# Per-head factors spread by one product for two heads, low-rank factors padded to 128 rows, and two smaller edits in a three-layer fp32 kernel

## The chip, the cores and the metric

The kernel runs as one program on one core of a Trainium2 chip. The metric is the device time of one execution in microseconds (us). PE is the engine of matrix products, DVE the vector engine, ACT the engine of activation functions, POOL the general engine, and SP a queue that only starts transfers (DMAs). Everything is in fp32 precision for 1024 tokens of 1024 features.

## The reference, cut to what matters

Three layers run one after another: a gated linear recurrence ("hawk"), an RWKV7 time mix, and a hybrid of a convolution and a diagonal state space (S5). The first two are each followed by a gated feed-forward part (FFN) and a per-layer embedding. Of the RWKV7 layer this matters here, with 16 heads of 64 features:

```python
w = w0 + tanh(xw @ w1) @ w2          # w1: 1024 x 64, w2: 64 x 1024
a = sigmoid(a0 + (xa @ a1) @ a2)     # a1: 1024 x 64, a2: 64 x 1024
g = sigmoid(xg @ g1) @ g2            # g1: 1024 x 160, g2: 160 x 1024
kk = k * k_k;  kk = kk / norm of kk over each head's 64 features
y = rwkv7_scan(r, decay(w), k, v, -kk, kk * a)     # token after token, per head
yn = (y - mean) * rsqrt(var + eps)                 # mean and variance over each head
out = ((yn * ln_w + ln_b) + bonus) * g @ w_o
```

The state space of the third layer takes `dt = exp(log_dt)`, one value for each of 32 groups. Each layer begins with `x * rsqrt(mean(x*x) + eps) * gain` over the 1024 features of a token.

## The kernel before, in words

Activations lie feature-major: a tile has 128 features on the partitions and 512 tokens (a "half") or 256 (a "segment") along it. A large product is three products in a row (mm3, lines L249, L250, L251), since each operand is split into two parts of 12 bits. Small products are plain fp32, and the trace then shows two records for each: a row with x2 is one product.

**Start.** Token rows of the input are loaded by SP in the order of the program, with some 25 small parameter rows (L204) between them, and transposed on PE (L356). The copies of the transposed tiles (L2130) are squared by ACT (L309, L312), and DVE adds eight squares (L313). PE sums them over the partitions (L273), DVE and POOL take the root (L289, L290), PE spreads the result (L281, in rstd_bcast), DVE multiplies (L328), and ACT and DVE split the result and the weights (L215, L216). Then the first products run. The second half of the tokens repeats this later.

**The woven stage** (some 1340 to 2420 us) is the RWKV7 layer. Generators yield steps, each with an engine and an estimated time, and a planner (weave_, L686) writes their instructions in one order for all engines. The engines then take them strictly in this order. Three kinds of work are woven: the projections (mm3 with 256 tokens; weights and activations prepared by DVE and ACT), the "finish" of each pair of heads and segment (8 pairs x 4 segments = 32 times), and the scan over 16 chunks of 64 tokens, with its closing part "post" for each chunk. Behind the scan comes the product with w_o.

In a finish the second low-rank factors are applied: lwD holds them in DRAM as three slots of 128 rows, w2 over a2 in slot 0, g2[0:128] in slot 1, and g2[128:160] on rows 96 to 127 of slot 2. fload (L931) loads a pair's part, and lora2 (L923) multiplies only the rows in use:

```python
zw = lora2(pz, lw, [(0, 0, 0, 64)])                # 64 rows
za = lora2(pz, lw, [(0, 0, 64, 128)])              # 64 rows
zo = lora2(pz, lw, [(1, 1, 0, P), (2, 2, 96, P)])  # 128 rows and 32 rows
```

The norm of kk: ACT squares k (L986), PE sums over each head (heads_sum, L1431) into one column per head with tokens on the partitions, DVE forms rn (L991, L992), and heads_bcast (L1434) spreads the factors back over 64 features each. Its stationary operand is one column, read 64 times; two products, one for each head, fill 128 output rows:

```python
self.nc.tensor.matmul(bc[64 * hd : 64 * hd + 64, c * P : (c + 1) * P],
                      x[:, 2 * c + hd : 2 * c + hd + 1].to_broadcast([P, 64]), self.ident,
                      start=True, stop=True)
```

L1003 writes t1 over the squared k, and L1007 multiplies t1 by the spread factors. In post the same helper spreads the root of the variance: PE centres y (L1303), ACT squares and copies (L1306, L1308), PE sums (L1431), DVE and POOL form the factor hr (L1315), heads_bcast spreads it with eight products, and DVE closes (L1319 to L1324).

**The end of the stage.** The last chunk has the inverse of small triangular blocks (DVE, L1146 and L1149), whose result goes through DRAM: SP stores it (L1157, four transfers) and loads it turned (L1168), and PE goes on with L1179. At about the same time s5_prep (L1444) begins: POOL issues its parameter loads (L1475 to L1481), the last two of which read every second element of log_dt into 64 partitions each.

Of the kernel before, what the change touches and what calls it, by code (L numbers as in the profile page):

```python
# [8 lines left out]
F32 = mybir.dt.float32  # L9
# [47 lines left out]
class Net:  # L57
    """Feature-major activations: tile [128 features, 512 tokens] per (k, half)."""
# [34 lines left out]
    def open_top(self):  # L93
        """One more pool above the group's, closed before them."""
# [4 lines left out]
    def open_rtop(self):  # L99
        """Another one, from the other end of the memory."""  # L100
# [44 lines left out]
    def s(self, dt=F32, n=HT):  # L145
        """scratch [128, n <= 516]"""
# [3 lines left out]
    def extra(self, tag, shape, dt, every, bufs):  # L150
        """now and then a slot of the pool on the right, where that is for more of the others"""
# [7 lines left out]
    def ld(self, src=None, n=HT, rows=P):  # L159
        """tile for a load; loads have slots of their own, for they run ahead"""  # L160
# [66 lines left out]
    def load_ws(self, srcs, nk, m, tag="w"):  # L227
        """srcs: DRAM APs arranged [p, nk, n] for columns c..c+n; returns hi, lo tiles [P, nk, m]"""
# [17 lines left out]
    def mm3(self, ps, w, x, first, last):  # L246
        """ps += w.T @ x with w = (hi, lo), x = (hi, lo)"""
# [5 lines left out]
    # W columns [c0, c0+128) for all nk row tiles  # L253
# [3 lines left out]
    def lin(self, w, xs, nk):  # L257
        """xs: list of (hi, lo) per k -> PSUM tile"""
# [6 lines left out]
    def rstd_bcast(self, acc, scale, eps, acc2=None):  # L265
        """acc [128, 512] -> PSUM [128, 512]: (sum over partitions * scale + eps)^-0.5 on all partitions; with acc2,
        for which that is the factor of another norm: that one and the product of both"""
# [25 lines left out]
        rs = root(sums(acc))  # L293
# [8 lines left out]
    def square(self, h, k, half, gain=None):  # L302
        """h[k][half] is final: its part of the sum of squares (and of that of the products with the gain)"""
# [54 lines left out]

    def load_T(self, src, nk, sink):
# [4 lines left out]
    def blocks(self, nblk, units, in_unit, post, nk_out, wout, h, add_bias=None, lag=2, delay=3, mid=None, late=None, fill=None, nlate=LATE):  # L364
        """units: weight items per block; in_unit(b, i, half, w) ; post(b, half) -> list of nk_out (hi, lo)"""
# [51 lines left out]
        # the first half of the last block before the second half of the one before it  # L417
# [34 lines left out]
    def hawk(self, h, xn, mid, late):  # L452
# [5 lines left out]
        # c8 = 8 softplus(-lam), softplus(z) = max(z, 0) + log1p(exp(-|z|)), log1p(e) = 2 atanh(e / (2 + e))  # L458
# [100 lines left out]
    def ple_prep(self, layer):  # L559
        """p, features on the partitions, split"""  # L560
# [40 lines left out]
    NSEG, SN = 4, 256  # token segments of the dense part  # L601

    def rwkv_consts(self):
# [7 lines left out]
        # block-diagonal ones (2 heads), identity minus the same / 64, and per-head selector columns  # L611
# [8 lines left out]
        # [s, t] masks on both heads: s < t | s <= t  # L620
# [1665 lines left out]
```

## Time and profile before

| | |
|---|---|
| three runs, us | 4186.73, 4188.85, 4215.79 |
| median, us | 4188.85 |
| span of the profiled execution, us | 4186.6 |
| busy PE / DVE / ACT / POOL, us | 3949.4 / 2544.7 / 1466.1 / 179.3 |
| mean granted clock of PE, share of full speed | 0.957 |

For the profiled execution the page gives its span, from the first to the last instruction, and no other time; the span is 0.13 us below the fastest of the three runs and 2.25 us below the median. PE is busy for 94% of the span. Times in the trace count from the span's start.

### The profile page before, as it was taken

The numbers are of one execution on the slowest core, as the hardware profiler recorded it, in microseconds if no ns is written. First come the engines' busy times: TensorE is split into PE (matmuls) and PEld (weight loads), VectorE is DVE, ScalarE is ACT, GpSimd is POOL, SyncE is SP. The second block draws the span as 40 slices with busy tenths as digits, with TensorE's granted clock in tenths as the row PEclk, the third lists the DMA queues.
The fourth block names the chain that finished last, engine by engine and source line by source line (L and its number), as shares of the span: only waits on it lengthen the run. The fifth ranks groups of instructions, "written<-read, shape, count | busy, mean of one in ns | idle before, by whom it ended". The sixth has DMA issues, their size and how long they took to land.

```text
span 4186.6 us, 58441 instructions
## 1 busy us (share of the span) xinstructions
PE 3949.4 (94%) x22510; PEld 3216.6 (77%) x22510; DVE 2544.7 (61%) x5192; ACT 1466.1 (35%) x2491; POOL 179.3 (4%) x376
## 2 busy tenths in 40 slices
PE   6998999999988999999999699999999999999899
PEld 5776788888877877777867587888887877888687
DVE  6665733333364678777756476354536599997655
ACT  4455511111132665554542241111113332222533
POOL 0000000000000000000000101010100000000000
PEclk8999999999998999989979799999999999999999
DMA  3111111111122789676776541212211244332775
GB/s 103 48 47 34 51 46 51 41 56 51 34 67 88 216 252 237 174 209 170 194 194 173 97 127 52 63 49 66 63 49 58 71 119 118 109 115 96 236 226 186
DMA packets 695830, 464.49 MB, mean 111 GB/s; under 512 B 197956, under 2 KB 620800, under 8 KB 695552
## 3 DMA queue, kind: packets, MB, share of 16 engines
q1 hardware_dynamic: 514272, 367.80, 30.0%
q10 hardware_dynamic: 175872, 83.90, 7.3%
q0 software_dynamic: 5408, 9.06, 1.1%
q8 instruction: 177, 2.90, 0.3%
q14 instruction: 101, 0.83, 0.1%
HBM read 355.51 MB, written 106.69 MB: 110 GB/s over the span
## 4 chain that ended last, share of the span: by engine, by line
PE 69%; DVE 12%; DMA 7%; ACT 5%; issue 4%; SPq 1%; POOL 1%; ACTq 0%; DVEq 0%; POOLq 0%
PE mm L249 15%; PE mm L251 14%; PE mm L250 14%; PE ob L249 4%; PE ob L250 4%; PE ob L251 4%; DVE cy L1882 3%; PE g L1100 2%; PE g L926 1%; PE g L1438 1%; PE y L1291 1%; DMA BK<-bkD 1%; PE y L1289 1%; DVE w L863 1%; PE mm L2073 1%
## 5 line engine op out<-in xcount | busy, mean ns | idle before, releaser
L249 PE MATMUL mm<-T,w 128*128 128x512 f32 (+1 forms) x2944 | 1152.6, 393 | 47.1 <-ACT w L215 22.5
L251 PE MATMUL mm<-T,w 128*128 128x512 f32 (+1 forms) x2944 | 1149.9, 391 | 9.6 <-DVE w L216 9.6
L250 PE MATMUL mm<-T,w 128*128 128x512 f32 (+1 forms) x2944 | 1150.3, 392 | 1.1 <-DVE T L1380 0.9
L249 PEld LDWEIGHTS mm<-T,w 128*128 128x128 f32 x2944 | 558.6, 190 | 174.3 <-ACT w L215 26.9
L251 PEld LDWEIGHTS mm<-T,w 128*128 128x128 f32 x2944 | 559.0, 190 | 126.8 <-DVE w L216 12.1
L250 PEld LDWEIGHTS mm<-T,w 128*128 128x128 f32 x2944 | 559.7, 190 | 117.5 <-DVE T L1380 1.7
L215 ACT CAST w<-wraw 128x1024 fp32r<-128x1024 f32 (+1 forms) x286 | 288.4, 1014 | 988.8 <-PE mm L250 700.2
L216 DVE TENSOR_TENSOR w<-wraw,w 128x1024 fp32r<-128x1024 f32 (+1 forms) x286 | 335.1, 1177 | 373.9 <-ACT w L215 371.1
L389 DVE TENSOR_TENSOR h<-ob,h 128x512 f32<-128x512 f32 x416 | 286.1, 690 | 230.7 <-PE ob L251 227.5
L249 PE MATMUL ob<-S,w 128*128 128x512 f32 x896 | 359.2, 401 | 21.7 <-DVE h L389 21.1
L1882 DVE SCALAR_TENSOR_TENSOR cy<-cu,pv,cy 128x512 f32<-128x512 f32 x480 | 350.9, 749 | 12.3 <-ACT cy L1880 2.6
L250 PE MATMUL ob<-S,w 128*128 128x512 f32 x896 | 354.7, 396 | 0.2 <-DVE S L216 0.2
L251 PE MATMUL ob<-S,w 128*128 128x512 f32 x896 | 354.7, 396 | 0.0
L249 PE MATMUL mm<-M,w 128*128 128x256 f32 x768 | 255.1, 332 | 16.4 <-ACT M L837 8.5
L250 PE MATMUL mm<-N,w 128*128 128x256 f32 x768 | 229.7, 299 | 4.4 <-DVE N L839 4.3
L251 PE MATMUL mm<-M,w 128*128 128x256 f32 x768 | 229.8, 299 | 4.3 <-DVE w L863 4.0
L249 PEld LDWEIGHTS ob<-S,w 128*128 128x128 f32 x896 | 169.9, 190 | 70.2 <-DVE h L389 30.2
L251 PEld LDWEIGHTS ob<-S,w 128*128 128x128 f32 x896 | 169.7, 189 | 38.6
L250 PEld LDWEIGHTS ob<-S,w 128*128 128x128 f32 x896 | 170.1, 190 | 36.3 <-DVE S L216 0.6
L249 PEld LDWEIGHTS mm<-M,w 128*128 128x128 f32 x768 | 157.0, 204 | 50.3 <-issue 23.3
L439 DVE TENSOR_TENSOR S<-mm,S 128x512 f32<-128x512 f32 x88 | 60.8, 690 | 211.7 <-PE mm L251 209.8
L215 ACT CAST S<-S 128x512 fp32r<-128x512 f32 x128 | 79.3, 620 | 266.3 <-DVE S L439 154.4
(458 smaller groups left out, 5431.9 us busy)
## 6 DMA issues: line engine op xcount, KB each, us to landing
wraw<-in_rw_w_rkv_dram ACTq DMA_DIRECT2D x96, 512.0 KB
wraw<-in_ffn_w_in_dram SPq DMA_DIRECT2D x88, 512.0 KB
wraw<-in_w_in_dram SPq DMA_DIRECT2D x48, 512.0 KB
wraw<-in_ffn_w_out_dram SPq DMA_DIRECT2D x44, 512.0 KB
BK<-bkD SPq DMA_DIRECT2D x64, 256.0 KB
wraw<-in_rw_w_o_dram ACTq DMA_DIRECT2D x24, 512.0 KB
wraw<-in_lru_w_in_dram SPq DMA_DIRECT2D x20, 512.0 KB
wraw<-in_ple_w_gate_dram SPq DMA_DIRECT2D x16, 512.0 KB
```

The source lines that it names most:

```text
L215: self.nc.scalar.copy(hi, x)
L216: self.nc.vector.tensor_sub(lo, x, hi.bitcast(F32))
L249: nc.tensor.matmul(ps, w[0], x[0], start=first, stop=False)
L250: nc.tensor.matmul(ps, w[0], x[1], start=False, stop=False)
L251: nc.tensor.matmul(ps, w[1], x[0], start=False, stop=last)
L389: nc.vector.tensor_add(h[m][half], ps, h[m][half])
L439: nc.vector.tensor_mul(a, ps, sg.pop((b, j, half)))
L863: nc.vector.tensor_sub(wl.rearrange(fl), r.rearrange(fl), wh.bitcast(F32).rearrange(fl))
L926: nc.tensor.matmul(ps, lw[r0:r1, slot, :], HW[hx][r0:r1], start=x == 0, stop=x == len(rows) - 1)
L1100: nc.tensor.matmul(g[:, 128 * x : 128 * x + 128], bk[rs, x].rearrange("p a b -> p (a b)"), qt[rs, j0 + x].rearrange("p a b -> p (a b)"), s ...
L1289: nc.tensor.matmul(o[rs], s[rs, x], qz[rs, j, 1, :], start=True, stop=False)
L1882: nc.vector.scalar_tensor_tensor(y, x[:, k : k + HT], cw(k), y, ALU.mult, ALU.add)
```

## The change

Four edits, in the words of the code:

- heads_bcast takes a factor that is already repeated over the 64 columns of each head, and does one product with a 128-column stationary for two heads. The repeated factor rx is written by a new DVE copy (128 x 256) in the finish, into the tile of the squared k, which t1 then overwrites; and by a new ACT copy (128 x 512) in post.
- lwD gets a fourth slot and zeros in the rows not in use, so that every product of lora2 has 128 rows. The activation behind g1's last columns now covers all 128 rows. A pair's load grows from 192 to 256 KB. The zeros go out as six transfers of SP from a tile that DVE clears.
- The two strided loads of log_dt go; two small DVE copies take the values from the tile that is loaded anyway.
- For the first norm of both halves, ACT squares the four tiles of token rows and sums each row in the same instruction (square_rows); the eight squares, seven additions and four sum products of each half go.

Comments also go from the file, so line numbers shift. The planner's constants stay, but for the costs of the changed steps.

```diff
-        rs = root(sums(acc))
+        rs = root(acc if acc.shape[-1] == 4 else sums(acc))
...
+    def square_rows(self, rows, half):
+        self.acc[half] = ss = self.tiny("ss", (P, 4), 2)
+        for c, r in enumerate(rows):
+            sq = self.wp.tile(list(r.shape), F32, tag="wh", name=self.n("sq"), bufs=self.nW[1])
+            self.nc.scalar.activation(sq, r, AF.Square, accum_out=ss[:, c : c + 1])
...
-               (5, w128(G1, 0), (AF.Sigmoid, 0, 128, 1)), (5, w128(G1, 32), (AF.Sigmoid, 96, 128, 2))]
+               (5, w128(G1, 0), (AF.Sigmoid, 0, 128, 1)), (5, w128(G1, 32), (AF.Sigmoid, 0, 128, 2))]
...
-        self.lwD = d((P, KD, 3, P), "lwD")
+        self.lwD = d((P, KD, 4, P), "lwD")
...
+            if src is None:
+                for y in (0, 4):
+                    nc.sync.dma_start(self.lwD[rows, y : y + 4, j], zero[rows].rearrange("p (j n) -> p j n", j=4))
...
-            for x, (slot, hx, r0, r1) in enumerate(rows):
-                nc.tensor.matmul(ps, lw[r0:r1, slot, :], HW[hx][r0:r1], start=x == 0, stop=x == len(rows) - 1)
+            for x, (slot, hx) in enumerate(rows):
+                nc.tensor.matmul(ps, lw[:, slot, :], HW[hx], start=x == 0, stop=x == len(rows) - 1)
...
-                    zo = lora2(pz, lw, [(1, 1, 0, P), (2, 2, 96, P)])
+                    zo = lora2(pz, lw, [(2, 1), (3, 2)])
...
-                    yield E("V", 0.2, rel=pz)
+                    yield E("V", 0.45, rel=pz)
...
+                    rx = sq.rearrange("p (a b) -> p a b", b=64)
                     nc.vector.reciprocal(rn, rn)
-                    pz = yield E("P", 1.0 * f, bank="g", par=True, use=0.9)
-                    pb = self.heads_bcast(rn, pz, n // P)
+                    nc.vector.tensor_copy(rx, rn.unsqueeze(2).to_broadcast([P, n // 64, 64]))
+                    pz = yield E("P", 0.25, bank="g", par=True, use=0.9)
+                    pb = self.heads_bcast(rx, pz, n // P)
...
-                ps = yield E("P", 1.04, bank="g", use=0.9)
-                b = self.heads_bcast(rs, ps)
+                yield E("A", 0.48)
+                rx = self.tiny("psq", (P, HT), 1).rearrange("p (a b) -> p a b", b=64)
+                nc.scalar.copy(rx, rs.unsqueeze(2).to_broadcast([P, 8, 64]))
+                ps = yield E("P", 0.5, bank="g", use=0.9)
+                b = self.heads_bcast(rx, ps)
...
-            for hd in range(2):
-                self.nc.tensor.matmul(bc[64 * hd : 64 * hd + 64, c * P : (c + 1) * P],
-                                      x[:, 2 * c + hd : 2 * c + hd + 1].to_broadcast([P, 64]), self.ident,
-                                      start=True, stop=True)
+            self.nc.tensor.matmul(bc[:, c * P : (c + 1) * P],
+                                  x[:, 2 * c : 2 * c + 2].rearrange("p a b -> p (a b)"), self.ident, start=True, stop=True)
...
-            for b in range(2):
-                dma(dt[64 * b : 64 * b + 64, 32:48], ldt[b:32:2].partition_broadcast(64))
...
+            nc.vector.tensor_copy(dt[lo, 32:48], dt[lo, 0:32:2])
+            nc.vector.tensor_copy(dt[hi, 32:48], dt[hi, 1:32:2])
...
+            net.square_rows(rows[0], 0)
             net.turn_rows(rows[0], KD, 0, sink)
```

In the program's order for PE, the first finish stands before as follows (L1438 is heads_bcast, L926 a lora2 product, L249 to L251 the projections beside it):

```order
L1431 MATMUL g_9935<-bsel,F_9882 128x2 x2
L249 MATMUL mm_9912<-M_9445,w_9863 128x256
L250 MATMUL mm_9912<-N_9446,w_9863 128x256
L251 MATMUL mm_9912<-M_9445,w_9864 128x256
L249 MATMUL mm_9912<-M_9497,w_9863 128x256
L250 MATMUL mm_9912<-N_9498,w_9863 128x256
L251 MATMUL mm_9912<-M_9497,w_9864 128x256
L1438 MATMUL g_9949<-ident,rn_9943 64x128 x4
L926 MATMUL g_9961<-HW_9198,l_9832 128x256
```

The same place on PE after the change (lora2 is L940, heads_bcast L1456):

```order
L1450 MATMUL g_9900<-bsel,F_9848 128x2 x2
L249 MATMUL mm_9891<-M_9407,w_9829 128x256
L250 MATMUL mm_9891<-N_9408,w_9829 128x256
L251 MATMUL mm_9891<-M_9407,w_9830 128x256
L940 MATMUL g_9913<-HW_9167,l_9801 128x256
L1456 MATMUL g_9916<-ident,F_9848 128x128 x2
```

Four products with 64 output rows became two with 128, three projection products later than the sums instead of six, and their stationary is now the tile F in place of the small rn.

On DVE the same finish, before (rn L991 and L992, the operands L997 and L1000, t1 L1003, t1 times the spread factors L1007):

```order
L991 TENSOR_SCALAR rn_9943<-g_9935 128x4
L992 RECIPROCAL rn_9943<-rn_9943 128x4
L997 SCALAR_TENSOR_TENSOR Qs_9954<-L_9744,nkk,F_9881 128x4x64
L1000 TENSOR_TENSOR Qs_9954<-L_9744,F_9881 128x4x64
L1003 SCALAR_TENSOR_TENSOR F_9882<-F_9879,L_9744 128x256
L863 TENSOR_TENSOR w_9930<-wraw_9790,w_9929 128x1024
L1007 SCALAR_TENSOR_TENSOR F_9882<-F_9882,hkk,g_9949 128x256
```

And on DVE after (the new copy is L1008, t1 is L1019):

```order
L1005 TENSOR_SCALAR rn_9909<-g_9900 128x4
L1007 RECIPROCAL rn_9909<-rn_9909 128x4
L1008 COPY F_9848<-rn_9909 128x256
L1013 SCALAR_TENSOR_TENSOR Qs_9919<-L_9713,nkk,F_9847 128x4x64
L1016 TENSOR_TENSOR Qs_9919<-L_9713,F_9847 128x4x64
L1019 SCALAR_TENSOR_TENSOR F_9848<-F_9845,L_9713 128x256
L979 SCALAR_TENSOR_TENSOR F_9930<-rm_8720,F_9884 128x260
L1023 SCALAR_TENSOR_TENSOR F_9848<-F_9848,hkk,g_9916 128x256
```

The copy stands between the reciprocal and the operands, and t1 now writes the tile F_9848 that the spreading product reads.

At the start of the program ACT has before (L2130 copies of turned tiles, L312 their squares):

```order
L2130 ACT_TABLE_LOAD
L2130 COPY h_162<-mm_157 128x512
L2130 COPY h_176<-mm_171 128x512
L312 ACTIVATE S_215<-h_169 128x512
L312 ACTIVATE S_218<-h_176 128x512
L2130 COPY h_190<-mm_185 128x512
L312 ACTIVATE S_221<-h_183 128x512
```

And after (L364 squares of token rows, L2149 the copies):

```order
L364 ACT_TABLE_LOAD
L364 ACTIVATE sq_158,ss_157<-ldT_89 128x1024
L364 ACTIVATE sq_160,ss_157<-ldT_91 128x1024
L364 ACTIVATE sq_162,ss_157<-ldT_93 128x1024
L364 ACTIVATE sq_164,ss_157<-ldT_95 128x1024
L2149 COPY h_171<-mm_166 128x512
L2149 COPY h_185<-mm_180 128x512
```

Four squares of twice the size stand ahead of the copies, where eight stood between and behind them.

## Rows read from the trace of the kernel before

**Rows 1.** Windows: busy us (instructions) of PE, PEld, DVE, ACT, POOL; clock; DMA share; GB/s
```profile
1340.00:1700.00 360.00, 327.54 (x2145) 276.44 (x2146) 260.45 (x640) 227.38 (x499) 22.00 (x70) 0.92 0.83 227
1700.00:2160.00 460.00, 446.12 (x5176) 362.01 (x5177) 333.55 (x1101) 234.29 (x536) 35.81 (x84) 0.92 0.69 184
...
500.00:630.00 130.00, 130.00 (x572) 107.04 (x571) 49.00 (x64) 26.09 (x35) 0.00 (x0) 1.00 0.18 53
```
**Rows 2.** Groups of PE by line and shape, 1340 to 2420: busy us, mean ns
```profile
L926 PE MATMUL g<-HW,l 64*128 64x256 f32 x128 | 47.0, 449 | 0.0
...
L1438 PE MATMUL g<-ident,rn 128*64 128x128 f32 x256 | 23.3, 308 | 0.8 <-DVE rn L992 0.7
```
**Rows 3.** Timeline of PE around lora2 products: start, duration, instruction, records
```profile
1443.62 0.28 PE L251 MATMUL mm<-M,w 128*128 128x256 f32 x1
1443.83 0.70 PE L926 MATMUL g<-HW,l 64*128 64x256 f32 x2
...
1444.68 0.28 PE L250 MATMUL mm<-N,w 128*128 128x256 f32 x1
...
1447.76 0.28 PE L251 MATMUL mm<-M,w 128*128 128x256 f32 x1
1447.88 1.22 PE L926 MATMUL g<-HW,l 128*128 128x256 f32 x4
...
1449.25 0.28 PE L250 MATMUL mm<-N,w 128*128 128x256 f32 x1
...
1458.97 0.28 PE L251 MATMUL mm<-M,w 128*128 128x256 f32 x1
1459.09 0.60 PE L1019 MATMUL g<-L,bo 128*128 128x256 f32 x2
...
1459.65 0.28 PE L250 MATMUL mm<-N,w 128*128 128x256 f32 x1
```
**Rows 4.** Timeline of PE around a transposition (L1216) and heads_bcast in post
```profile
2327.26 0.28 PE L251 MATMUL mm<-XO,w 128*128 128x256 f32 x1
2327.38 0.60 PE L1216 MATMUL g<-ident,BK 128*128 128x128 f32 x4
...
2327.94 0.28 PE L250 MATMUL mm<-XO,w 128*128 128x256 f32 x1
...
2335.10 0.28 PE L251 MATMUL mm<-XO,w 128*128 128x256 f32 x1
2335.30 1.09 PE L1438 MATMUL g<-ident,hr 128*64 128x128 f32 x16
...
2336.55 0.28 PE L250 MATMUL mm<-XO,w 128*128 128x256 f32 x1
```
**Rows 5.** A group of DVE in the finish: busy, mean ns | idle before, releaser
```profile
L1007 DVE SCALAR_TENSOR_TENSOR F<-F,hkk,g 128x256 f32<-128x256 f32 x32 | 15.3, 478 | 7.1 <-PE g L1438 6.8
```
**Rows 6.** A group of ACT in post
```profile
L1308 ACT COPY PY<-g 128x512 f32<-128x512 f32 x16 | 9.4, 585 | 0.0
```
**Rows 7.** Timeline of POOL, SP and PE at the stage's end, with [idle before <-releaser]
```profile
2338.20 1.66 POOL L1481 DMA_DIRECT2D pv<-in_ssm_log_dt_dram  x2
...
2340.65 21.20 SPq L1157 DMA_DIRECT2D yiD<-YB  x4
...
2367.25 0.31 PE L1179 MATMUL g<-XT,AM 32*32 32x32 f32 x2 [26.58 <-DVE XT L1173]
```
**Rows 8.** The line L1481 alone: its transfers from issue to landing
```profile
DMA to landing us min/median/max: 13.2/18.0/22.9
```
**Rows 9.** Timeline of PE at the start and at the second half's first norm
```profile
26.29 1.87 PE L273 MATMUL ms<-ones,L 128*128 128x1 f32 x8 [5.57 <-DVE L L313]
...
40.67 0.50 PE L251 MATMUL mm<-T,w 128*128 128x512 f32 x1 [2.22 <-DVE w L216]
...
60.00 1.05 PE L273 MATMUL ms<-ones,L 128*128 128x1 f32 x8 [0.48 <-DVE L L313]
...
65.05 1.00 PE L249 MATMUL mm<-T,w 128*128 128x512 f32 x2 [1.26 <-ACT T L215]
```

More of the change, by code (lines that the diff above doesn't have):

```diff
@@ L642, in rwkv_consts @@
         self.vD = d((16, P, KD, 64), "vD")
-        self.lwD = d((P, KD, 3, P), "lwD")
+        self.lwD = d((P, KD, 4, P), "lwD")
         I = self.I
-        for j, rows, src in ((0, slice(0, 64), I["rw_w2"][0]), (0, slice(64, P), I["rw_a2"][0]),
-                             (1, slice(0, P), I["rw_g2"][0][0:P]), (2, slice(0, 96), I["rw_g2"][0][0:96]), (2, slice(96, P), I["rw_g2"][0][P : P + 32])):
-            nc.sync.dma_start(self.lwD[rows, :, j], src.rearrange("p (j n) -> p j n", j=KD))
+        zero = self.s()
+        nc.vector.memset(zero, 0.0)
+        for j, rows, src in ((0, slice(0, 64), I["rw_w2"][0]), (0, slice(64, P), None), (1, slice(0, 64), None),
+                             (1, slice(64, P), I["rw_a2"][0]), (2, slice(0, P), I["rw_g2"][0][0:P]),
+                             (3, slice(0, 96), None), (3, slice(96, P), I["rw_g2"][0][P : P + 32])):
+            if src is None:
+                for y in (0, 4):
+                    nc.sync.dma_start(self.lwD[rows, y : y + 4, j], zero[rows].rearrange("p (j n) -> p j n", j=4))
+            else:
+                nc.sync.dma_start(self.lwD[rows, :, j], src.rearrange("p (j n) -> p j n", j=KD))
         self.EdA = c((P, KD, 20), "EdA")
@@ L935, in fload @@
                         sig=[("fl", x)], par=True)
-                raw = self.top.tile([P, 3, P], F32, tag=f"l2{x % nld}", name=self.n("l2"), bufs=1)
+                raw = self.top.tile([P, 4, P], F32, tag=f"l2{x % nld}", name=self.n("l2"), bufs=1)
                 nc.sync.dma_start(raw, self.lwD[:, j])
@@ L948, in finish @@
                     x_ = seg * KD + j
-                    pz = yield E("P", 0.87 * f, wait=[("fl", x_)], bank="g", use=0.5)
+                    pz = yield E("P", 0.87 * f, wait=[("fl", x_)], bank="g")
                     lw, k, r, v = FL.pop(x_)
-                    zw = lora2(pz, lw, [(0, 0, 0, 64)])
+                    zw = lora2(pz, lw, [(0, 0)])
                     sg = fs(65 * nch)
@@ L956, in finish @@
                     nc.scalar.activation(c65(sg)[:, :, 1:], c65(sg)[:, :, 1:], AF.Copy, bias=0.5, scale=0.5)
-                    pz = yield E("P", 0.87 * f, bank="g", use=0.5)
-                    za = lora2(pz, lw, [(0, 0, 64, 128)])
+                    pz = yield E("P", 0.87 * f, bank="g")
+                    za = lora2(pz, lw, [(1, 0)])
                     yield E("A", AE, rel=pz, par=True)
@@ L967, in finish @@
                     nc.vector.tensor_sub(c65(csm), c65(cs), c65(cs)[:, :, 32:33].to_broadcast([P, nch, 65]))
[L968 to L969 removed]
+                    pz = yield E("P", 1.74 * f, bank="g", sig=[("fin", seg, j)])
+                    zo = lora2(pz, lw, [(2, 1), (3, 2)])
                     yield E("A", AE, rel=pz, par=True)
@@ L1471, in main @@
         def main():
-            yield E("S", 9, 1.22, wait=list(wait))
+            yield E("S", 7, 1.22, wait=list(wait))
             rows = small()
@@ L1487, in main @@
             nc.vector.tensor_copy(li, pt[:, 48:96])
+            yield V(16)
+            nc.vector.tensor_copy(dt[lo, 32:48], dt[lo, 0:32:2])
+            yield V(16)
+            nc.vector.tensor_copy(dt[hi, 32:48], dt[hi, 1:32:2])
             yield A()
@@ L2157, in second @@
             def second():
+                net.square_rows(rows[1], 1)
                 net.turn_rows(rows[1], KD, 1, sink)
```

1 line of the change is left out of this document (removed).

## The prediction

> **What bounds the kernel now.** I read the page first: PE is busy for 3949.4 of 4186.6 us, so time can be won in two ways, by less work on PE where PE is dense, and by ending waits in the few places where PE stands still. Next came the windows by stage, since the share of 94% is a mean. In the first half of the woven stage PE is busy for 327.54 of 360 us, DVE for 260.45, and the DMA engines for 0.83 of the time; in the second half PE is busy for 446.12 of 460 us [rows 1]. In both the granted clock is 0.92, a mix of PE's two levels, 2.4 and 1.2 GHz. So in the second half a us taken from PE should come off nearly whole, in the first half somewhat less. Then the timelines of PE, to see what a small product costs between projections: not its duration, because records overlap, but the start of the last projection product ahead of it to the start of the second one behind it. Last the places where PE waits long: the program's start [rows 9] and the end of the woven stage, where one wait is 26.58 us [rows 7].
>
> **The change part by part.** The sum is made from the profiled execution, whose span is 4186.6 us, 2.25 us below the median of the runs; all terms are differences, and they are taken from the median, 4188.85.
>
> *Padded lora2 products.* A 64-row product takes PE from 1443.62 to 1444.68, 1.06 us; a product of the same 256 tokens with all 128 rows (L1019) from 1458.97 to 1459.65, 0.68 us [rows 3]. What differs is the number of rows: on each side of the partial product PE moves between two row forms. Each padded product so saves 0.38 us. The group has 128 records, two for each product [rows 2], so 64 products: 24.3 us. The pair with 128 and 32 rows takes from 1447.76 to 1449.25, 1.49 us [rows 3]; a plain start follows the one before by 0.12 us (1458.97 to 1459.09), so one full product adds 0.68 - 0.24 = 0.44 us to two plain starts, and two of them would take 0.24 + 2 x 0.44 = 1.12 us. That saves 0.37 us, 32 times: 11.8 us.
>
> *One product for two heads.* In post the eight small products (16 records) take from 2335.10 to 2336.55, 1.45 us. Four records with full 128 columns take from 2327.26 to 2327.94, 0.68 us, of which 0.24 is again two plain starts, so 0.44 us for four records [rows 4]. The four full products that take their place, eight records, then take 0.24 + 2 x 0.44 = 1.12 us, which saves 0.33, 16 times: 5.3 us. In the finish four products (256 records in 32 finishes [rows 2]) become two. By the same rows, two full products add 0.44 us to the plain starts; four half ones, at half of the 1.45 - 0.24 us that eight add and the other half of the change of form, some 0.77. That is 0.33 us, 32 times: 10.6 us.
>
> Together 52.0 us of PE. Two reasons make it less. The change of form is paid only where a neighbour is full: the order of PE has 592 changes of form after the edit and 812 before, 220 fewer, and the 144 groups that I counted have 288 edges, so 52.0 x 220/288 = 39.7 us. And PE is not always what ends last: half of the groups lie in each half of the stage, where PE is busy 0.91 and 0.97 of the time [rows 1], so 39.7 x 0.94 = 37 us. I take 37. Bounds: 18, if only the second half keeps its share, and 60, if the removed edges cost in the slow clock as well, where everything on PE takes longer.
>
> One page of the Trainium skill speaks against the padding: in TensorE: Matmul & The Clock Gate, the table under "Why this matters for your kernels" has a single product with 32 rows taking as long as one with 128. By that the padding wins nothing and the PE term would be 11. Another page of the Trainium skill, TensorEngine Tiling (Array Packing), says under Key Properties that a change of the tiling mode drains the engine; the 1.06 us against 0.68 [rows 3] agree with this one.
>
> *log_dt.* POOL issues the two strided loads at 2338.20; SP's four stores of L1157, which carry the last chunk's triangles, start at 2340.65 and take 21.20 us to issue, and PE's next product stands 26.58 us idle [rows 7]. The strided loads land up to 22.9 us after issue [rows 8], near 2361, and the issue of the four stores ends at 2361.85. I read this as the stores queued behind the loads' elements. Four issues at the 0.83 us that each of POOL's two takes [rows 7] are 3.3 us, so up to 21.20 - 3.3 = 17.9 us come off, and of the wait some 9 us stay: the last store's landing, the load L1168, the turn and DVE's step, of which 5.4 us lie behind the stores even now. I take 17. Bounds 10, if the other parameter loads of POOL or the stores' own landing fill part of the gap, and 18.
>
> The Trainium skill puts another size on this. Its page DMA: Bandwidth & Descriptors says under Rules for kernel authors that a strided last dimension gives one descriptor per element; with the 10.5 ns per packet of the page's section Measured, an estimate for 1024 elements on 16 engines is 0.67 us for each load, 1.3 us for both. By that the term would be 1; the 22.9 us of [rows 8] don't agree.
>
> *First squares.* In the first half PE waits 5.57 us for DVE's additions and spends 1.87 us on the sums [rows 9]; both go, and the squares of the rows can run before the tiles are turned. That is 7.4 us, if nothing else holds the first product: PE's wait for the split weights (2.22 us at 40.67) stands behind DVE's queue of multiplications, which moves up with it [rows 9]. In the second half the sums cost 0.48 + 1.05 us and the wait at 65.05 another 1.26, so up to 2.8 us [rows 9]. Together 10 us; bounds 6, if parameter loads hold the multiplications, and 13.
>
> *Added work.* 32 copies on DVE of 128x256, at most the 0.478 us of a two-operand instruction of that size [rows 5], 15.3 us; 16 copies on ACT of 128x512 at 0.585 us [rows 6], 9.4 us. DVE is free for 99 us and ACT for 133 us of the stage's first half [rows 1], which hides them, as long as PE has projection products to do meanwhile; without that cover all 24.7 us would show. I take 2 for the few that fall on the closing chunks, with bounds 0 and 24.7. In the finish DVE's t1 now waits for the spreading product, which reads the tile that t1 overwrites; queued behind it on DVE are the split of the weights and L1007's successor, for which PE waits in turn. Today L1007 waits only 6.8 us for heads_bcast in all [rows 5], so this wait is counted at nothing. The zeros for lwD make SP wait for a DVE instruction near the end of the first layer, with FFN weights queued behind on SP; from 500 to 630 PE is busy for 130.00 of 130 us [rows 1], so that the loads have room, and it costs nothing. The 2 MB that the four-slot loads add are in the rival below.
>
> Sum: 10 + 37 + 17 - 2 = 62, so 4188.85 - 62 = 4127 us.
>
> **The rivals.** (a) The PE term is given back. In the first half DMA is at 0.83 and DVE at 260 of 360 us [rows 1]; if loads and their preparation end last there, as 32 larger l2 loads make likelier, PE only waits longer. Then the half of the term that lies there goes and the second half's is 18, and the loads cost 6 (2 MB at the stage's 227 GB/s is 9 us of transfer, most of it hidden): 10 + 17 + 18 - 6 = 39, some 4150 us. For it: the DMA share; against it: PE's 0.91.
>
> (b) The clock. Full products for half-empty ones could raise the granted clock, 0.92 over 820 us [rows 1], so that 66 us are lost now. Half of this back is 33 us: 4127 - 33 = 4094 us. Against it: busy shares of 0.91 and 0.97 go with the same 0.92 [rows 1], so a denser PE alone did not raise it.
>
> (c) Something else holds the stores of L1157, say the other parameter loads that POOL issues just before, and the strided loads are only late with them: the log_dt term is 0 instead of 17, 4144 us. Against it: the loads' landing and the end of the stores lie within 1 us of each other [rows 7, 8]. The estimate by the Trainium skill's page, above, would bring it about.
>
> (d) The 0.38 us belong to the operands (a wait for the loaded factors, a first read of them), not to the row form. Then the padding does nothing, and only the spreading products count, 15.9 of the 52.0 us: 15.9 x 37/52.0 = 11, and 10 + 17 + 11 - 2 = 36, 4153 us. Against it: both forms stand between the same neighbours without a wait [rows 2, 3]. The Trainium skill's table on TensorE, above, would have it so.
>
> (e) Slower: t1's wait. DVE is in order. If the spreading product is late in PE's order, t1 stops DVE and with it the split of weights on which the next projection rests. It outweighs the rest from 62/32 = 1.9 us of exposed wait in each finish; at 3 us it is 96 us, and 4188.85 - 62 + 96 = 4223 us. For it: the product stands only after the sums, the copy and three projection products; against it: two DVE instructions of some 0.45 us lie between copy and t1, and what PE has to do until then is some 1.1 us, a lora2 product and the three beside it [rows 3].
>
> **How the numbers follow.** A measurement of this kernel can tell about 1% from no change, 41.9 us: faster is below 4147. The forecast has 0.56, (a) 0.17, (b) 0.14, (c) 0.05, (d) 0.04, (e) 0.04. The forecast's own bounds, taken together, reach from 4098 to 4150. (b) extends the range below, to 4085, (a) and (d) above, to 4158; outside are (e) and the tails of the others. Faster: the forecast, (b), (c) and, as it lies at the border, 0.05 of (a), 0.80; same: the rest of (a) and (d), 0.16; slower 0.04.
>
> **What would show it.** In the profile after: lora2 groups with 128*128 alone and 0.68 us from start to start; heads_bcast with half the records; PE's wait ahead of the small 32-row products at the stage's end near 9 us and the four stores of SP near 2 us; the first L251 near 33 us. The forecast is wrong if the windows 1340 to 2160 keep their length while PE's busy time falls (a), if the mean clock there rises above 0.95 (b), if the wait at the stage's end stays above 20 us (c), or if DVE's t1 shows idle time on the spreading product (e).

## The result, and the profile after

The changed kernel takes 4152.75 us (median of four runs, 4135.10 to 4155.62) against 4187.79 for the kernel before (four runs). The medians lie 35 us apart. The recorded ratio, which is not the quotient of the medians, is 0.9892 with a 95% interval from 0.9852 to 0.9931, so 29 to 62 us are won; the text goes by the medians. The time lies in the predicted range (4085 to 4158), with 62 us forecast and 35 measured. By the prediction's own border, 4147 us, it counts as the same, to which the prediction gave 0.16.

The profiled execution of after has a span of 4153.6 us, 33.0 less than that of before. To see where they lie, both spans are cut at the same five places in the work: a product of L249 in the first layer (the 101st), the first projection of the woven stage, its last product with w_o, an early product of the FFN behind it, and the end. The windows of before (busy us and instructions of PE, PEld, DVE, ACT, POOL; clock; DMA share; GB/s):

```profile
0.00:152.50 152.50, 115.46 (x472) 91.68 (x473) 91.80 (x171) 70.08 (x104) 4.20 (x16) 0.88 0.29 88
152.50:1351.90 1199.40, 1145.05 (x4951) 925.75 (x4949) 568.99 (x786) 354.66 (x486) 10.16 (x16) 0.98 0.17 51
1351.90:2339.80 987.90, 937.22 (x9024) 769.79 (x9025) 700.86 (x2094) 512.60 (x1131) 69.97 (x169) 0.91 0.72 197
2339.80:2434.50 94.70, 49.25 (x352) 40.04 (x351) 33.15 (x57) 27.30 (x49) 3.37 (x6) 0.62 0.60 123
2434.50:4186.30 1751.80, 1702.45 (x7718) 1389.29 (x7716) 1149.91 (x2086) 501.43 (x723) 91.65 (x170) 0.99 0.35 105
```

The same five stretches of after:

```profile
0.00:130.40 130.40, 103.83 (x456) 83.79 (x457) 82.90 (x157) 70.25 (x103) 4.19 (x16) 0.93 0.33 100
130.40:1333.60 1203.20, 1148.61 (x4951) 928.17 (x4949) 569.71 (x787) 354.49 (x486) 11.06 (x16) 0.98 0.17 51
1333.60:2315.60 982.00, 890.24 (x8777) 766.46 (x8778) 701.83 (x2113) 517.36 (x1146) 70.16 (x167) 0.93 0.73 200
2315.60:2395.40 79.80, 49.66 (x343) 40.94 (x343) 35.65 (x72) 28.20 (x50) 3.32 (x5) 0.64 0.49 146
2395.40:4153.30 1757.90, 1707.60 (x7717) 1395.49 (x7716) 1149.33 (x2086) 501.46 (x723) 91.74 (x170) 0.99 0.35 104
```

The start is 22.1 us shorter, the layers up to the woven stage 3.8 longer, the woven stage 5.9 shorter, its end 14.9 shorter, and the rest 6.1 longer: 33.0. The third stretch is the surprise. PE's busy time fell by 47.0 us (937.22 to 890.24), and PE's idle time rose by 41.1 (50.7 to 91.8). The second and fifth stretches are outside the change; in the profiles of before and of the twelve kernels below the fifth takes 1748.0 to 1756.7 us with the same work, so its 6 us are scatter between executions. Each profile is one execution, and a difference of some 10 us between two profiles can be such scatter.

The single prices of the padded products came as forecast. The timeline of PE in after, around one padded product and around the pair for g, which answers to [rows 3]:

```profile
1446.89 0.28 PE L251 MATMUL mm<-M,w 128*128 128x256 f32 x1
1447.01 0.59 PE L940 MATMUL g<-HW,l 128*128 128x256 f32 x2
...
1447.56 0.28 PE L250 MATMUL mm<-N,w 128*128 128x256 f32 x1
...
1449.11 0.28 PE L251 MATMUL mm<-M,w 128*128 128x256 f32 x1
1449.23 1.02 PE L940 MATMUL g<-HW,l 128*128 128x256 f32 x4
...
1450.21 0.28 PE L250 MATMUL mm<-N,w 128*128 128x256 f32 x1
```

From start to start that is 0.67 us (1.06 before) and 1.10 us (1.49 before). The start of the program and the end of the stage, from the timeline of after, answer to [rows 7] and [rows 9]:

```profile
33.43 0.79 PE L251 MATMUL mm<-T,w 128*128 128x512 f32 x1 [0.16 <-DVE w L216]
...
2318.79 2.51 SPq L1173 DMA_DIRECT2D yiD<-YB  x4
...
2328.25 1.43 PE L1195 MATMUL g<-XT,AM 32*32 32x32 f32 x32 [11.84 <-DVE XT L1189]
```

The first L251 starts 7.2 us earlier, SP's four stores are issued in 2.51 us instead of 21.20, and PE's wait behind them is 11.84 us instead of 26.58. What holds PE in the woven stage of after is spread over many waits; the list of them up to the first product with w_o, largest sums first (total, times, longest one):

```profile
PE g L1450 <- ACT F L1000: 9.7, 9, 2.5
PE g L1195 <- DVE XT L1189: 9.1, 6, 3.6
PE g L1222 <- DMA V<-vD: 8.2, 2, 5.9
PE mm L249 <- ACT M L851: 8.0, 7, 5.0
PE g L1035 <- issue: 7.9, 3, 4.4
PE mm L251 <- DVE w L877: 7.6, 13, 0.8
```

ACT, DVE, a load and PE's own issue: no releaser has more than 10 of the 86 us that PE is idle there (44 in before). The largest sum in before is

```profile
PE mm L249 <- ACT M L837: 8.5, 7, 5.5
```

### The profile page after: what moved, and what is told of

It is laid out like the page before. It is cut to its first block, busy times and chain, and to the rows that moved or that the text cites. A ratio compares the mean times of both kernels' runs of the same rounds, so it can differ in the third digit from the quotient of the medians.

```text
span 4153.6 us, 57970 instructions
## 1 busy us (share of the span) xinstructions
PE 3899.9 (94%) x22238; PEld 3214.8 (77%) x22238; DVE 2539.4 (61%) x5213; ACT 1471.8 (35%) x2507; POOL 180.5 (4%) x374
## 4 chain that ended last, share of the span: by engine, by line
PE 67%; DVE 13%; DMA 8%; issue 5%; ACT 5%; SPq 1%; POOL 1%; ACTq 0%; DVEq 0%; POOLq 0%
PE mm L249 14%; PE mm L251 14%; PE mm L250 14%; PE ob L249 4%; PE ob L250 4%; PE ob L251 4%; DVE cy L1901 3%; PE g L1116 1%; DVE w L877 1%; PE g L940 1%; DMA BK<-bkD 1%; PE y L1307 1%; PE mm L2091 1%; PE mm L2092 1%; PE g L1456 1%
## 5 line engine op out<-in xcount | busy, mean ns | idle before, releaser
L249 PE MATMUL mm<-T,w 128*128 128x512 f32 (+1 forms) x2944 | 1152.9, 393 | 48.7 <-ACT w L215 27.4
L251 PE MATMUL mm<-T,w 128*128 128x512 f32 (+1 forms) x2944 | 1149.2, 391 | 4.5 <-DVE w L216 4.5
L249 PEld LDWEIGHTS mm<-T,w 128*128 128x128 f32 x2944 | 559.3, 190 | 174.5 <-ACT w L215 31.7
L251 PEld LDWEIGHTS mm<-T,w 128*128 128x128 f32 x2944 | 559.3, 190 | 121.6 <-DVE w L216 6.4
L249 PE MATMUL ob<-S,w 128*128 128x512 f32 x896 | 359.7, 402 | 20.4 <-DVE h L396 19.6
L251 PE MATMUL ob<-S,w 128*128 128x512 f32 x896 | 355.2, 396 | 0.0
L249 PE MATMUL mm<-M,w 128*128 128x256 f32 x768 | 259.0, 337 | 13.7 <-ACT M L851 8.0
L251 PE MATMUL mm<-M,w 128*128 128x256 f32 x768 | 227.3, 296 | 7.7 <-DVE w L877 7.6
L249 PEld LDWEIGHTS ob<-S,w 128*128 128x128 f32 x896 | 170.2, 190 | 68.9 <-DVE h L396 28.1
L251 PEld LDWEIGHTS ob<-S,w 128*128 128x128 f32 x896 | 169.8, 190 | 39.0
L249 PEld LDWEIGHTS mm<-M,w 128*128 128x128 f32 x768 | 154.4, 201 | 28.1 <-ACT M L851 10.8
```

The costliest lines, as they stand in the source:

```text
L249: nc.tensor.matmul(ps, w[0], x[0], start=first, stop=False)
L251: nc.tensor.matmul(ps, w[1], x[0], start=False, stop=last)
```

## The experiments

Each kernel was timed in rounds beside the kernel before, with a profile. Times are medians; R is the recorded ratio to before with its 95% interval, and not the quotient of the medians. Before stood at 4189.28, 4188.56 and 4189.91 us in the three sets, so that medians of different sets may be compared; with 4 to 12 runs of each kernel and the intervals of R, a difference of two medians is good to 10 us or somewhat more. Unless said otherwise an edit is made in the kernel after. "Forms" are the rows and columns that PE's products use; an "order" is what the planner writes for all engines from its costs.

**e1_small: the two small edits alone.** The code of heads_bcast, lora2 and lwD with their callers is that of before again, for instance

```diff
-            for x, (slot, hx) in enumerate(rows):
-                nc.tensor.matmul(ps, lw[:, slot, :], HW[hx], start=x == 0, stop=x == len(rows) - 1)
+            for x, (slot, hx, r0, r1) in enumerate(rows):
+                nc.tensor.matmul(ps, lw[r0:r1, slot, :], HW[hx][r0:r1], start=x == 0, stop=x == len(rows) - 1)
```

> The kernel before with only the squares from rows and the log_dt copies; lora2, lwD and heads_bcast as before, so the order of the woven stage is that of before. Theory 1 (the product edits gave nothing in the end: PE's busy time in the woven stage fell by 47 us and its idle time rose by 41): about 35 us faster than before, as fast as the whole change, some 4152. Rival (the product edits gave their 37 us and something else ate them elsewhere): 27 us faster at most, 10 + 17, some 4160.

Measured: 4150.76 us, R 0.9917 (0.9895 to 0.9938). Its windows for the woven stage and for the end of it:

```profile
1330.20:2317.60 987.40, 928.91 (x9025) 762.89 (x9026) 701.29 (x2094) 513.29 (x1131) 69.91 (x167) 0.92 0.73 197
2317.60:2392.70 75.10, 48.61 (x352) 40.07 (x351) 33.41 (x59) 27.30 (x49) 3.29 (x5) 0.64 0.53 156
```

The woven stage is as long as before (987.9), its end 19.6 us shorter, the start 21.6 us. So, within the noise, the two small edits alone account for all that the whole change gave, and the product edits end at nothing. That much is theory 1; why is left to the next kernels.

This kernel also tests what held SP's stores. POOL issues the last of its other parameter loads 3.2 us ahead of the stores (at 2315.44 and 2318.60), as in before (3.0 us, at 2337.64 and 2340.65); only the two strided loads are missing, and the issue of the four stores takes 2.89 us instead of 21.20:

```profile
2318.60 2.89 SPq L1164 DMA_DIRECT2D yiD<-YB  x4
```

**e3_narrow: the forms of before in the order of after.** Copies, loads and the order on every engine are those of after.

```diff
-                nc.tensor.matmul(ps, lw[:, slot, :], HW[hx], start=x == 0, stop=x == len(rows) - 1)
+                r = (slice(0, 64), slice(64, P), slice(0, P), slice(96, P))[slot]
+                nc.tensor.matmul(ps, lw[r, slot, :], HW[hx][r], start=x == 0, stop=x == len(rows) - 1)
...
+            for hd in range(2):
+                self.nc.tensor.matmul(bc[64 * hd : 64 * hd + 64, c * P : (c + 1) * P], x[:, 2 * c + hd, :], self.ident,
+                                      start=True, stop=True)
```

> The kernel after, with its order, its copies and its loads, but every padded product multiplies only the rows that are not zero (64, 64, 128, 32) and the spreading is done by two products of 64 columns for two heads again, so that only the forms of PE's products are those of before. If PE's work sets the pace in the order of after (theory A): 37 to 50 us slower than the kernel after, some 4190 to 4200. If something else sets the pace there (theory B: waits for DMA, ACT and DVE take up what PE saves): within 10 us of the kernel after.

Measured: 4196.31 us, R 1.0013 (0.9997 to 1.0029), 44 us above the kernel after. The woven stage:

```profile
1334.40:2375.60 1041.20, 954.43 (x9025) 777.36 (x9026) 702.38 (x2113) 519.06 (x1146) 68.39 (x167) 0.90 0.70 189
```

In this order PE's work does set the pace, as theory A says: 64 us more of busy PE make the profiled stage 59 us longer (this profile is the slowest of the twelve runs, 17 us above their median). With the old forms the stage is 53 us longer here (1041.2) than in before (987.9), but that puts two things together, the order and the added copies and loads. With the added work in both, the order alone is the difference to e6_old_narrow, below: 27 us by the medians with the old forms, and 5 us with the new ones (after against e4_oldorder).

**e4_oldorder: the new work in the order of before.** The planner is given the costs of before at the changed steps, which puts back the order of before on every engine; the copies stand in it.

```diff
-                    pz = yield E("P", 0.25, bank="g", par=True, use=0.9)
+                    pz = yield E("P", 1.0 * f, bank="g", par=True, use=0.9)
...
-                ps = yield E("P", 0.5, bank="g", use=0.9)
+                ps = yield E("P", 1.04, bank="g", use=0.9)
```

(and likewise the shares of lora2, the 0.45 of DVE, and post's step for ACT.)

> The kernel after, but with the planner's costs of the kernel before at the changed steps, so that every engine's order in the woven stage is that of before, with the two copies put in. If the new order lost what the products gave (theory A, order): some 30 us faster than the kernel after, about 4120, and the woven stage from the first projection to the last product with w_o 35 us shorter than before. If something other than PE sets the pace in any order (theory B): within 10 us of the kernel after.

Measured: 4147.67 us, R 0.9905 (0.9885 to 0.9924), 5 us below the kernel after: theory A fails in this form, and the time lies within the 10 us of theory B, which e3_narrow had not borne out. The old order doesn't bring out the saving either. The woven stage:

```profile
1327.50:2304.50 977.00, 892.10 (x8777) 765.50 (x8778) 708.36 (x2126) 518.24 (x1146) 71.89 (x167) 0.93 0.74 201
```

Compared with e1_small in the same order, PE is busy 36.8 us less and idle 26.4 us more, so the profiled stage is 10.4 us shorter; the medians differ by 3 us only.

**e6_old_narrow: the old order and old forms with the added work.** The edits of e3_narrow in e4_oldorder.

> The kernel e4_oldorder (the old order with the new copies, loads and small edits), but with the old forms of PE's products again (64, 64, 128 and 32 rows; two spreading products of 64 columns). e1_small has the same order and old forms without the added work, and took 4150.8 us; e4_oldorder 4147.7. Theory O (an order is written for the costs it was given, so cheaper products leave waits in it, and the added work is nearly free): within 15 us of e4_oldorder, 4148 to 4163. Theory W (the forms give their 40 us in any order, and the copies, the wait of t1 and the larger loads take them back): 37 to 45 us slower than e4_oldorder, some 4190.

Measured: 4169.63 us, R 0.9942 (0.9916 to 0.9968); its ten runs reach from 4146 to 4186. That is 22 us above e4_oldorder, so the forms are worth some 22 us in the old order, and 19 above e1_small, so the added work costs some 19, though with this scatter it can be a few us or 30. It lies between the two theories: a part of the forms' gain never arrives, and the added work takes the rest. The profiled stage:

```profile
1328.80:2340.00 1011.20, 946.32 (x9025) 772.76 (x9026) 709.09 (x2126) 520.26 (x1146) 69.78 (x167) 0.91 0.72 195
```

Against e1_small PE has 17 us more busy time with the same products; the clock is 0.91 instead of 0.92, which over 1000 us is 10 of them.

The four kernels lead step by step from the small edits to the whole change: the added work costs 19 us (e1_small to e6_old_narrow), the new forms win 22 (to e4_oldorder), the new order costs 5 (to after). That is the 2 us by which after lies above e1_small.

**e5_ownrx: t1 without its wait.** The spread factors of the finish get a tile of their own.

```diff
-                    rx = sq.rearrange("p (a b) -> p a b", b=64)
+                    rx = self.tiny("rx", (P, n // 64, 64), 1)
```

> The kernel after, with the spread factors of the finish in a tile of their own, so that t1 no longer waits for the spreading product. In the trace of after t1 waits 14.1 us in all for it. If these waits hold the stage (theory C): some 14 us faster than the kernel after. If they lie in DVE's slack: within 5 us of it, and t1's wait moves to the multiplication behind it.

Measured: 4149.58 us, R 0.9913 (0.9891 to 0.9934): 3 us below the kernel after, within the noise, where theory C says 14. t1's group in the DVE groups of after (busy, mean ns | idle before it, releaser) is

```profile
L1019 DVE SCALAR_TENSOR_TENSOR F<-F,L 128x256 f32<-128x256 f32 x32 | 13.5, 422 | 14.2 <-PE g L1456 14.1
```

and in e5_ownrx the wait stands before the next instruction (L1023, 5.6 us). That fits slack on DVE and not theory C, and e13_own, below, says the same.

**e9_twocopies: the new DVE copy made twice.**

```diff
+                    for _ in range(2):
                         nc.vector.tensor_copy(rx, rn.unsqueeze(2).to_broadcast([P, n // 64, 64]))
```

> The kernel after, with the new DVE copy of the finish made twice, 32 x 0.295 us = 9.4 us of DVE work more in the path from the sums to the spreading product. If that path or DVE sets the pace (theory W): 9 us slower or more. If it is hidden: within 4 us.

Measured: 4153.70 us, R 0.9911 (0.9884 to 0.9937), 1 us above the kernel after. By the medians the copy is hidden, but the noise doesn't exclude the 9 us of theory W, and the profiled stage is 8.9 us longer than that of after:

```profile
1328.60:2319.50 990.90, 895.34 (x8777) 770.79 (x8778) 710.19 (x2145) 517.42 (x1146) 70.13 (x167) 0.93 0.72 199
```

So the price of these copies isn't measured to better than their own 9.4 us.

**e8_traffic: 8 MB more of transfers.** Nothing waits for them, but SP has 32 more to issue.

```diff
                 nc.sync.dma_start(raw, self.lwD[:, j])
+                nc.sync.dma_start(self.dram.tile([P, 4, P], F32, name=self.n("dump")), self.lwD[:, j])
```

> The kernel after, with a further transfer of 256 KB from DRAM to DRAM behind each of the 32 loads of low-rank factors, 8 MB in all, which nothing waits for. If the DMA engines set the pace of the stage (theory D: 66 MB at some 228 GB/s are the 290 us of its first part in every kernel so far): 8 MB at that rate, some 36 us slower, and the first part 10 to 15 us longer. If latencies and orders set it: under 8 us slower.

Measured: 4168.69 us, R 0.9954 (0.9935 to 0.9973), 16 us above the kernel after; its twelve runs reach from 4159 to 4188. That is half of what a stage bound by transfers would show, and twice what a stage without regard to them would. The profiled execution, 12 us above the median, has a longer stage than that:

```profile
1329.70:2346.60 1016.90, 913.66 (x8777) 787.41 (x8778) 702.75 (x2113) 517.36 (x1146) 66.25 (x167) 0.90 0.73 202
```

It is 34.9 us longer than in after, about what theory D says, though 23.4 of them are busy time of PE with the same products at a clock of 0.90 instead of 0.93. So transfers count, and how far they bound the stage isn't settled. At 16 to 35 us for 8 MB, the 2 MB that the four-slot loads add would cost 4 to 9 us: a part of e6_old_narrow's 19. What makes up the rest of the 19 wasn't separated.

**e7_costs: after with truer costs for two steps.** All work is the same; only the order changes.

```diff
-                    pz = yield E("P", 0.25, bank="g", par=True, use=0.9)
+                    pz = yield E("P", 0.44, bank="g", par=True, use=0.9)
...
-                ps = yield E("P", 0.5, bank="g", use=0.9)
+                ps = yield E("P", 0.88, bank="g", use=0.9)
```

> The kernel after, with the planner's costs of the two spreading steps set from 0.25 and 0.5 us to what the trace shows for two and four full products beside projections, 0.44 and 0.88 us; all engines' work is the same, in another order. Theory O (the order decides how much of PE's saving arrives): the woven stage changes by more than 5 us, faster if the truer costs make a better order, 4125 to 4145. Theory B (a pace set by DMA, ACT or DVE in the stage's first part): no change beyond 5 us.

Measured: 4127.76 us, R 0.9836 (0.9808 to 0.9864), 25 us below the kernel after, and by chance within 1 us of the time that was predicted for after. Its windows for the woven stage and its end, and PE's products that waited 11.84 us in after, from its timeline:

```profile
1335.10:2308.50 973.40, 889.75 (x8829) 762.42 (x8831) 710.05 (x2128) 519.07 (x1148) 74.84 (x168) 0.94 0.74 203
2308.50:2376.30 67.80, 42.00 (x301) 34.77 (x295) 31.87 (x56) 27.00 (x48) 2.84 (x4) 0.70 0.53 163
```

```profile
2304.47 0.22 PE L1195 MATMUL g<-XT,AM 32*32 32x32 f32 x2 [0.27 <-DVE XT L1189]
```

The stage changes by more than 5 us, as theory O says: it is 8.6 us shorter than in after and its end 12.0. In this order the last chunk's triangles are ready while products with w_o still run, and the wait is gone. Theory B, no change beyond 5 us, fails.

**e12_costs33 and e11_costs60: the same two costs at other values.** 0.33 and 0.66 in the one, 0.60 and 1.20 in the other, with the lines of e7_costs.

> The kernel after with the planner's costs of the two spreading steps at 0.33 and 0.66 us, between those of after (0.25 and 0.50: 4152) and e7_costs (0.44 and 0.88: 4128), and all work the same. Theory O1 (truth of the costs counts): between the two, 4133 to 4148. Theory O2 (dice): not between them, or as far off as e11_costs60.

> The kernel after with the planner's costs of the two spreading steps at 0.60 and 1.20 us, more than the trace shows (0.44 and 0.88), and all work the same. If the true costs are what makes the order of e7_costs good (theory O1): slower than e7_costs, 4135 or more. If any new order is a throw of the dice by some 20 us (theory O2): anywhere from 4120 to 4165, without regard to the distance from the true costs.

Measured: 4164.68 us, R 0.9929 (0.9904 to 0.9953), for 0.33; 4155.56 us, R 0.9909 (0.9886 to 0.9932), for 0.60. With the same work, the times over the cost are 4152.75 (0.25), 4164.68 (0.33), 4127.76 (0.44) and 4155.56 (0.60). The kernel between the first and the third is the slowest, so theory O1 falls for 0.33; theory O2, dice, fits all four. Of e12_costs33, where PE's busy share of the stage is the lowest of the four, 0.903, the stage and its end:

```profile
1330.80:2325.60 994.80, 898.12 (x8777) 769.01 (x8778) 705.37 (x2107) 517.93 (x1146) 74.77 (x167) 0.93 0.72 198
2325.60:2409.00 83.40, 50.74 (x343) 41.51 (x343) 37.27 (x78) 28.19 (x50) 3.34 (x5) 0.63 0.47 139
```

For 0.60 both theories hold. That the true cost gave the best of four orders may itself be chance.

**e10_narrow_lora: the padding undone in the good order.** The first of the two edits of e3_narrow, in e7_costs.

> The kernel e7_costs in its order and with its loads, but each lora2 product multiplies only the rows that are not zero (64, 64, 128 and 32), while the spreading keeps its full products: the padding alone is undone. The sum of single prices for it is 24.3 + 11.8 = 36 us of PE. If the row form is what costs (theory A): 25 to 40 us slower than e7_costs, 4153 to 4168. If the padding does nothing (the rival in which the 0.38 us belong to the operands): within 6 us, 4122 to 4134.

Measured: 4142.34 us, R 0.9881 (0.9856 to 0.9905), 15 us above e7_costs, where 36 us of single prices and 25 to 40 were expected. Neither theory is met; the row form costs, but 0.4 of its price arrives. The profiled stage:

```profile
1331.20:2317.00 985.80, 915.48 (x8835) 752.32 (x8837) 712.08 (x2128) 520.67 (x1148) 73.64 (x168) 0.94 0.72 201
```

PE is busy 25.7 us more than in e7_costs and idle 13.3 less, and the stage is 12.4 longer. Here the trade between work and waits is seen with all else equal.

**e13_own: e7_costs with the tile of e5_ownrx.**

> The kernel e7_costs with the spread factors of the finish in a tile of their own, so that t1 doesn't wait for the spreading product. After e5_ownrx (2 to 3 us below the kernel after, inside the noise) all theories expect little: 4118 to 4130. More than 8 us faster would say that t1's wait is on the path in the better order.

Measured: 4125.53 us, R 0.9842 (0.9814 to 0.9869): the same time as e7_costs. Both beat the kernel before by 1.6% and the kernel after by some 25 us.

## Why the prediction was right, and where its size was off

The direction and the range were right; the sum 10 + 37 + 17 - 2 was not, and that the time came to lie in the range is in part luck. In the same terms the runs show 22 for the start, 15 for log_dt, 22 for the forms, 19 lost by the added work and 5 by the order: 22 + 15 + 22 - 19 - 5 = 35, each good to some 10 us. Misses of both signs stand against each other. The measured 4152.75 also lies above the forecast's own bounds (4098 to 4150); it is in the range because rivals (a) and (d) extended it to 4158. Nor do those bounds follow from those of the terms: with the lowest of each, 6 + 18 + 10 - 24.7 = 9, the upper end is 4180.

The largest miss is in the work on PE, where 37 - 2 us were forecast and, net of the added work and the order, nothing came. Three steps of it failed.

The first is the 52.0 x 220/288 = 39.7 us. The single prices held: 0.67 and 1.10 us from start to start were forecast as 0.68 and 1.12. PE's busy time fell by 47 us, which seems to bear out the 39.7, but the clock rose with it. Busy time times granted clock, an estimate of PE's work at full clock, is 937.22 x 0.91 = 853 us in before and 890.24 x 0.93 = 828 us in after, 25 us less. By the same estimate, which the two digits of the clock leave uncertain by some 5 us, the other kernels whose stage stands above have 855 to 861 us with the old forms, 822 to 836 with the new, and 861 with the padding alone undone. So by this estimate the forms save some 25 us of work, and the rest of the 47 is the clock.

The second is "half of the groups lie in each half of the stage, where PE is busy 0.91 and 0.97 of the time, so 39.7 x 0.94 = 37 us". A busy share is not the share of a saving that arrives. With the order fixed, the forms were worth 44 us in the order of after (e3_narrow, where the clock fell from 0.93 to 0.90), 22 in that of before (e6_old_narrow against e4_oldorder), and the padding 15 of 36 in that of e7_costs. And the order was not fixed: the edit gave the planner new costs, and four orders with the same work spread over 37 us (4127.76 to 4164.68). Of the saving in PE's busy time 41 us came back as idle time, in which no single releaser stands out. The prediction counted the changes of form in the new order, but took no price for the order itself.

The third is the added work, counted at 2 us, with bounds 0 and 24.7. e6_old_narrow puts it at 19 in the old order, with a wide scatter. By the medians in the order of after, the DVE copy (e9_twocopies) and t1's wait (e5_ownrx) have no clear part in it, and the larger loads perhaps 4 to 9 us.

The term of the start was sized 10 us and is 22; the kernels with this edit take 128.5 to 135.1 us for the first stretch, against 152.5 in the one profile of before. The first L251 moved 7.2 us, as forecast (7.4). The rest lies in the second half. The windows of the same products, from the first of L249 on, of before:

```profile
33.80:100.30 66.50, 52.48 (x208) 40.73 (x209) 47.65 (x73) 36.87 (x57) 1.02 (x1) 0.86 0.17 49
```

and of after:

```profile
29.20:77.30 48.10, 44.01 (x200) 35.86 (x201) 34.80 (x54) 32.43 (x51) 1.02 (x1) 0.95 0.32 89
```

DVE is busy 12.9 us less in the window; the seven additions that are gone are 4.8 of it, and the rest is work that now lies ahead of the window or behind it. The prediction counted the waits at the sums [rows 9], not what was queued behind the second half's squares and additions: PE's waits for ACT's readings of the first products (L486, L490) fell from 4.6 to 1.7 us, and those for the split weights of DVE from 3.4 to 0.2. PE's idle time fell by 9.9 us here, and PE was busy 8.5 us less, 1.05 of it the sums [rows 9] and the rest the same products at a clock of 0.95 instead of 0.86, which the prediction didn't count either.

The term of log_dt was right: 17 forecast, 14.9 measured at the stage's end in after and 19.6 in e1_small. The reading behind it, that SP's stores wait for the strided loads, is borne out by the 2.51 us, and 2.89 in e1_small, that the four issues take without them.

Of the rivals, (a) gave 4150 us, 3 from the measured time, and its sign was seen: the stage kept its length while PE's busy time fell. Its cause was not shown. Transfers do count (e8_traffic), by how much isn't settled, and e7_costs wins 25 us with the same transfers, so that they alone don't set the time of after. (b), the clock, has its mechanism: in one order it is 0.90 with the old forms and 0.93 with the new (e3_narrow and after), 0.91 and 0.93 in another (e6_old_narrow and e4_oldorder), and 0.94 with and without padding in the third (e10_narrow_lora and e7_costs). So in two of the three a part of what the forms are worth comes by way of the clock; against before it rose by 0.02, not beyond the 0.95 that was the sign of (b), and this too went into waits. (c) falls with the 2.89 us of e1_small. (d) gave 4153 us, the nearest of all, and this is luck: its mechanism falls with e10_narrow_lora and e3_narrow, where the same operands cost more time in the old row form. Of (e) the sign was seen, 14.1 us of t1's idle time on the spreading product, but it cost nothing that e5_ownrx could show.

What stays open: why one order is better than another by up to 37 us, beyond the wait at the stage's end; what the old order pays for the added work; and how far transfers bound the stage.

## What to carry to other kernels

Where a planner writes the order, an edit to the work is two edits: price the work in a fixed order (keep the old costs, or the old forms in the new order), and then draw several orders before judging; here the draw was worth as much as the edit. A saving on an engine that is 94% busy arrived here in part only; the idle time that took its place shows in a window of the stage, not in the shares of the whole. When busy times of two profiles are compared, look at the granted clock beside them: of the 47 us that PE seemed to save here, some 22 were the clock by the estimate above. Look first for single long waits: two transfers of 4 KB and the squares of the first norm gave, within the noise, all that this change gave.

## What the runs showed of the hardware

- Two loads of every second 4-byte element, 4 KB each, took up to 22.9 us to land [rows 8] and held four stores of another queue: 21.20 us of issue with them, 2.51 (after) and 2.89 (e1_small) without.
- A product of 256 tokens with 64 rows costs 1.06 us between products with 128 rows, with zeros in the other 64 rows 0.67 us: more arithmetic, less time. Undoing the padding alone made the kernel 15 us slower (e10_narrow_lora).
- ACT's square with a sum along the row takes 1.06 us for 128x1024 and a second record of 0.19 us that reads the sum:

```profile
4.34 1.06 ACT L364 ACTIVATE sq<-ldT 128x1024 f32<-128x1024 f32 x1 [2.25 <-DMA ldT<-in_x_dram]
...
5.30 0.19 ACT L364 ACTIVATION_READ_ACCUMULATOR sq<-ldT 128x1 f32 x1
```
